# Seven products for eight in the FFN down projections of a two-layer decoder trunk

## The chip, the cores and the metric

One core of a Trainium2 chip runs the whole program. Five engines work side by side, each through its own queue in a fixed order: PE (matrix products), DVE (elementwise work), ACT (elementwise functions and copies), POOL (elementwise work) and SP (which issues DMA transfers). The metric is the device time of one execution in microseconds, as the median of several runs.

## The reference

The input is 512 tokens of width 1024 in float32. Two layers follow each other. Each is a mixer (attention in layer 0, causal pooling in layer 1) and then a SwiGLU feed-forward network (FFN), each between two RMS norms with a residual sum:

```python
def swiglu(h, w_gate, w_up, w_down):
    return (jax.nn.silu(h @ w_gate) * (h @ w_up)) @ w_down
...
        u = rmsnorm(h, g[2])
        h = h + rmsnorm(swiglu(u, ffn_w_gate[layer], ffn_w_up[layer], ffn_w_down[layer]), g[3])
```

The hidden width FFN_HIDDEN is 2816, which is 22 chunks of 128. The down projection is thus the product of a 512 x 2816 matrix of activations with a 2816 x 1024 matrix of weights.

## The kernel before

Every product is made from split numbers: `hi` is the operand rounded to fp32r, `lo` is the rest, and one product is three matmuls (hi by hi, hi by lo, lo by hi). To split one 128 x 512 tile, `conv` (line 242) lets ACT copy it into `hi` (line 244), and then DVE or POOL subtracts into `lo` (line 245). The engine of the subtraction comes from a pattern in CFG: the key `wlo` has 'ggv' (POOL, POOL, DVE) from the first FFN on, the key `slo` has 'v' (always DVE). `split` (line 219) is the same with DVE always.

An FFN has two parts. The gate and up projections (`Ffn.run`, `pair_weights`, `begin`, `middle`, `end`, `up_done`) go over 11 pairs of hidden chunks, first gate, then up for each pair, and already use a seven-product scheme: DVE combines weight blocks (line 913), ACT and DVE split them (lines 244, 245), PE multiplies with 256 columns at a time (lines 944 to 946), DVE puts the results together (lines 962 to 972) and makes the activations (lines 985 to 987). Two PSUM tags, psA and psS, with two banks each, hold these products.

The down projection follows (`down`, lines 776 to 813). It runs over two column halves n of 512. For each half it goes over the chunks, and in each chunk over the four token tiles of 128; one such step is three matmuls of 512 columns (lines 782 to 784), so 22 x 2 x 4 x 3 = 528 matmuls in a layer. Half 0 collects in the tags psT and psO, half 1 in psA and psS. Each weight tile is loaded, split once and used for four token tiles; each activation chunk is split once (`get`, line 1020). The last eight chunks of half 1 are kept back in a function `tail(t)`, which finishes token tile t, so that the norm of tile t (`post_norm`, line 815) can begin while PE works on tile t+1. In layer 0 the tails stand in the hand-written order `tr2` (line 62) with the pooling mixer: T is a tail, E is `Pool.enter` (post norm, then rows for the pooling), B the band matmuls (line 1126), M the mixing, F, R, A and Z prepare the next FFN, W its first weights. Before all of that `Pool.prepare` (line 1073) loads and scales the mixer's constants, lines 1079 and 1089 on DVE. In layer 1 the four tails are followed by the last norm and the store.

Tiles come from rotating groups by tag: `wq` (14 tiles of split weights), `wr` (11 raw weight tiles), `xe` (4), `g` (31, the general one), `jk` (2), `sc` (2). A tile can be written again only when its last reader is done. The order inside each engine's queue is set at build time by a planner that follows program order as priority and takes what is ready in its own time model.

## Time and profile before

| | |
|---|---|
| median of 3 runs | 1072.53 us (1071.33 to 1073.2) |
| the profiled execution | 1071.16 us |
| its span | 1069.4 us |
| PE busy | 1023.3 us, 96% |
| DVE busy | 755.3 us, 71% |
| ACT busy | 563.0 us, 53% |
| POOL busy | 314.5 us, 29% |

The span runs from the first to the last instruction. Times in the rows below count from the start of the span. Busy shares are means over stages that differ much from each other, so each stage is read by itself. Layer 0's down projection lies between 553 and 673 us, layer 1's between 943 and 1063 us.

### The profile page before, as it was taken

The numbers are of one execution on the slowest core, as the hardware profiler recorded it, in microseconds if no ns is written. First come the engines' busy times: TensorE is split into PE (matmuls) and PEld (weight loads), VectorE is DVE, ScalarE is ACT, GpSimd is POOL, SyncE is SP. The second block draws the span as 40 slices with busy tenths as digits, with TensorE's granted clock in tenths as the row PEclk, the third lists the DMA queues.
The fourth block names the chain that finished last, engine by engine and source line by source line (L and its number), as shares of the span: only waits on it lengthen the run. The fifth ranks groups of instructions, "written<-read, shape, count | busy, mean of one in ns | idle before, by whom it ended". The sixth has DMA issues, their size and how long they took to land.

```text
span 1069.4 us, 19004 instructions
## 1 busy us (share of the span) xinstructions
PE 1023.3 (96%) x6892; PEld 940.4 (88%) x6892; DVE 755.3 (71%) x1527; ACT 563.0 (53%) x1194; POOL 314.5 (29%) x282
## 2 busy tenths in 40 slices
PE   6999999997999999999999999988999999999997
PEld 5788978896888999999988888988999999978886
DVE  5338898758749999899973153998898898881204
ACT  6437688769656454454564352764444354472401
POOL 5713666767751000000026371420000000053510
PEclk9999999999999999999999999998999999999999
DMA  8841201323531434433343374003342333433302
GB/s 244 195 96 40 60 21 32 95 73 102 169 89 31 119 109 116 123 102 107 119 153 114 106 218 110 21 11 92 97 138 83 112 114 90 139 117 121 108 1 78
DMA packets 156493, 108.58 MB, mean 102 GB/s; under 512 B 14836, under 2 KB 137584, under 8 KB 156400
## 3 DMA queue, kind: packets, MB, share of 16 engines
q1 hardware_dynamic: 155600, 106.23, 34.6%
q8 instruction: 54, 0.88, 0.4%
q10 hardware_dynamic: 800, 1.15, 0.3%
q14 instruction: 39, 0.32, 0.1%
HBM read 101.88 MB, written 2.10 MB: 97 GB/s over the span
## 4 chain that ended last, share of the span: by engine, by line
PE 77%; DVE 8%; ACT 5%; issue 3%; DMA 3%; POOL 2%; SPq 1%; DVEq 0%; POOLq 0%; ACTq 0%
PE psS L944 8%; PE psS L945 8%; PE psS L946 7%; PE psA L944 5%; PE psA L945 5%; PE psA L946 5%; PE psT L784 2%; PE psO L784 2%; PE psT L782 2%; PE psT L783 2%; PE psO L783 2%; PE psO L782 2%; PE psA L782 2%; PE psA L784 2%; PE psA L783 2%
## 5 line engine op out<-in xcount | busy, mean ns | idle before, releaser
L244 ACT ACTIVATE wh<-wr 128x512 fp32r<-128x512 f32 x376 | 226.3, 626 | 256.8 <-DVE wr L913 82.4
L245 POOL TENSOR_TENSOR wl<-wr,wh 128x512 fp32r<-128x512 f32 x101 | 145.4, 1449 | 556.5 <-ACT wh L244 329.8
L245 DVE TENSOR_TENSOR wl<-wr,wh 128x512 fp32r<-128x512 f32 x275 | 189.5, 706 | 92.1 <-ACT wh L244 89.4
L944 PE MATMUL psS<-th,wh 128*128 128x256 f32 x528 | 149.8, 285 | 1.3 <-DVE comb L964 1.3
L945 PE MATMUL psS<-tl,wh 128*128 128x256 f32 x528 | 150.0, 285 | 0.0
L946 PE MATMUL psS<-th,wl 128*128 128x256 f32 x528 | 149.9, 284 | 0.0
L944 PEld LDWEIGHTS psS<-th,wh 128*128 128x128 f32 x528 | 101.6, 193 | 1.6 <-DVE comb L964 0.9
L945 PEld LDWEIGHTS psS<-tl,wh 128*128 128x128 f32 x528 | 101.8, 193 | 0.0
L946 PEld LDWEIGHTS psS<-th,wl 128*128 128x128 f32 x528 | 101.7, 193 | 0.0
L913 DVE TENSOR_TENSOR wr<-wr,wr 128x512 f32<-128x512 f32 x132 | 86.7, 682 | 1.3 <-DMA wr<-in_ffn_w_up_dram 0.5
L946 PE MATMUL psA<-uh,wl 128*128 128x256 f32 x272 | 77.5, 286 | 3.1 <-DVE wl L245 3.0
L944 PE MATMUL psA<-uh,wh 128*128 128x256 f32 x272 | 77.5, 286 | 2.1 <-DVE comb L962 1.7
L945 PE MATMUL psA<-ul,wh 128*128 128x256 f32 x272 | 77.3, 284 | 0.0
L270 POOL TENSOR_SCALAR E<-E,ri 128x128 f32<-128x128 f32 (+3 forms) x48 | 56.0, 1167 | 38.8 <-DVE ri L590 12.9
L584 ACT ACTIVATE E<-E,mn 128x128 f32<-128x128 f32 (+1 forms) x96 | 53.4, 557 | 15.7 <-DVE mn L582 15.0
L946 PEld LDWEIGHTS psA<-uh,wl 128*128 128x128 f32 x272 | 52.6, 194 | 3.5 <-DVE wl L245 3.5
L944 PEld LDWEIGHTS psA<-uh,wh 128*128 128x128 f32 x272 | 52.5, 193 | 2.7 <-DVE comb L962 2.1
L332 PE MATMUL psA<-uh,wh 128*128 128x512 f32 (+1 forms) x136 | 51.4, 378 | 1.7 <-DVE nq L464 1.5
L945 PEld LDWEIGHTS psA<-ul,wh 128*128 128x128 f32 x272 | 52.6, 193 | 0.0
L221 DVE TENSOR_TENSOR pl<-psT,ph 128x512 fp32r<-128x512 f32 (+1 forms) x72 | 42.3, 593 | 12.5 <-ACT ph L220 8.7
L334 PE MATMUL psA<-uh,wl 128*128 128x512 f32 (+1 forms) x136 | 50.9, 374 | 0.0
L333 PE MATMUL psA<-ul,wh 128*128 128x512 f32 (+1 forms) x136 | 50.7, 373 | 0.0
(354 smaller groups left out, 3009.8 us busy)
## 6 DMA issues: line engine op xcount, KB each, us to landing
wr<-in_ffn_w_gate_dram SPq DMA_DIRECT2D x98, 256.0 KB
wr<-in_ffn_w_up_dram SPq DMA_DIRECT2D x98, 256.0 KB
wr<-in_ffn_w_down_dram SPq DMA_DIRECT2D x88, 256.0 KB
wr<-in_attn_w_in_dram SPq DMA_DIRECT2D x40, 256.0 KB
wr<-in_attn_w_out_dram SPq DMA_DIRECT2D x16, 256.0 KB
x<-in_x_dram SPq DMA_DIRECT2D x4, 512.0 KB
gbc<-in_norm_g_dram SPq DMA_DIRECT2D x8, 256.0 KB
h<-in_x_dram SPq DMA_DIRECT2D x4, 512.0 KB
```

The costliest lines, as they stand in the source:

```text
L244: nc.scalar.activation(hi, src, AF.Copy)
L245: next_engine(key).tensor_tensor(lo, src, r32(hi), op=ALU.subtract)
L270: (nc.vector if k == "v" else nc.gpsimd).tensor_scalar(e, e, s1, None, op0=ALU.mult)
L332: nc.tensor.matmul(psum, wh, ah, start=first, stop=False)
L584: nc.scalar.activation(e, e, AF.Exp, bias=mn[:, n_:n_ + 1], scale=-1.0, accum_out=sm[:, n_:n_ + 1])
L782: nc.tensor.matmul(o, acts[c][0][:, tok], wh[k], start=first, stop=False)
L783: nc.tensor.matmul(o, acts[c][0][:, tok], wl[k], start=False, stop=False)
L784: nc.tensor.matmul(o, acts[c][1][:, tok], wh[k], start=False, stop=last)
L913: next_engine("sadd").tensor_tensor(o, x0, x1, op=op)
L944: nc.tensor.matmul(o, wh, bh, start=start and k == 0, stop=False, skip_group_check=True)
L945: nc.tensor.matmul(o, wh, bl, start=False, stop=False, skip_group_check=True)
L946: nc.tensor.matmul(o, wl, bh, start=False, stop=k == 3, skip_group_check=True)
```

## The change

Both down projections are rewritten as the method of the new class function `down(self, pairs)`. The tokens are cut into halves of 256, the hidden chunks into an even and an odd one of each pair, and the columns into halves of 512. Eight block products of a pair become seven (Strassen's scheme in Winograd's form). The first pass makes four products for each of the 11 pairs and collects them in four groups of two PSUM banks: C11 (psO), U (psT), C21 (psA), C12 (psS). Then the sums `u2` and `c22` are formed. The second pass makes the other three products of a pair and adds them onto C11, C21 and C12. The second-pass products of the last three pairs (`nres`) are kept back for the tails.

The scheme needs sums of blocks: three of half a tile for the activations (`act_sums`, made for the first six pairs, `npre`, already during the gate and up projections), four of weights, one more of activations. All splits of this stage use the key `slo`, so DVE makes every `lo`. Apart from this, the tag `sc` goes into `jk` (now 3), `g` has 33 tiles, and the two PSUM tags of the pooling mixer change places.

```diff
-    ng=31,
+    ng=33,
-    jk=2,
+    jk=3,
+    nres=3,
+    npre=6,
-    ptags=(('psO', 'psA'), ('psO', 'psS')),
+    ptags=(('psO', 'psS'), ('psO', 'psA')),
...
     def SC():
-        return T([P, S], "sc", 2, F32, "sc")
+        return JK("sc")
...
                     up_done(todo[i][0], ms[i - 1], ms[i])
+                    if pairs.index(todo[i][0]) < CFG["npre"]:
+                        self.act_sums(todo[i][0])
...
-            return down(get, NF, w_down[self.layer], lambda i: take)
+            return self.down(pairs)
+
+        def act_sums(self, p):
+            e, o = self.acts[2 * p], self.acts[2 * p + 1]
+            a11, a21, a22 = e[:, 0:256], e[:, 256:], o[:, 256:]
+            t_ = G([P, S], label="as")
+            s1, s3 = t_[:, 0:256], t_[:, 256:]
+            nc.vector.tensor_add(s1, a21, a22)
+            nc.vector.tensor_sub(s3, a11, a21)
+            nc.vector.tensor_sub(a21, s1, a11)
+            self.S[p] = t_
+
+        def down(self, pairs):
...
+            for i, p in enumerate(pairs):
+                if p not in self.S:
+                    self.act_sums(p)
+                b11, b12, b22 = raw(p, 0, 0), raw(p, 0, 1), raw(p, 1, 1)
+                t1, t2s[p] = JK("t1"), G([P, S], label="t2")
+                e_ = XE([P, 2, S], F32R, label="ae")
+                s_ = XE([P, 2, S], F32R, label="as")
+                conv(e_[:, 0, :], e_[:, 1, :], self.acts[2 * p], "slo")
+                w11 = put(b11)
+                sub(t1, b12, b11)
+                sub(t2s[p], b22, t1)
+                w2 = put(t2s[p])
+                sub(b12, b22, b12)
+                conv(s_[:, 0, :], s_[:, 1, :], self.S[p], "slo")
+                w3 = put(b12)
+                w1 = put(t1)
+                ends = i == 0, i == len(pairs) - 1
+                for o, a, c0, b in ((C11, e_, 0, w11), (U, e_, 256, w2), (C21, s_, 256, w3), (C12, s_, 0, w1)):
+                    for j in range(2):
+                        prod(o, (a[:, 0, c0:c0 + 256], a[:, 1, c0:c0 + 256]), b, j, *ends)
+            u2, c22 = [], []
+            for j in range(2):
+                x_ = G([P, S], label="u2")
+                nc.scalar.activation(x_, C11[j], AF.Copy)
+                nc.vector.tensor_add(x_, U[j], x_)
+                y_ = G([P, S], label="c22")
+                nc.vector.tensor_add(y_, C21[j], x_)
+                nc.vector.tensor_add(y_, C12[j], y_)
...
+            def second(p, keep):
+                b21, b22 = raw(p, 1, 0), raw(p, 1, 1)
...
+                w21 = put(b21, alloc)
...
+                conv(oh, ol, o, "slo")
+                sub(t2s[p], b21, t2s[p])
+                w4 = put(t2s[p], alloc)
+                sub(e[:, 256:], o[:, 0:256], e[:, 256:])
+                conv(s_[:, 0, :], s_[:, 1, :], e[:, 256:], "slo")
+                w22 = put(b22, alloc)
...
+            for p in pairs[:-R]:
+                for o, a, b in second(p, False):
+                    for j in range(2):
+                        prod(o, a, b, j)
+            held = [second(p, True) for p in pairs[-R:]]
+
+            def tail(t):
+                j = t % 2
+                for i, (p2, p4, p3) in enumerate(held):
+                    for x in ((p4,) if t >= 2 else (p2, p3)):
+                        prod(x[0], x[1], x[2], j, False, i == R - 1)
+                y_ = C([P, S], label="c12") if t < 2 else u2[j]
+                nc.vector.tensor_add(y_, (C12 if t < 2 else C21)[j], u2[j])
+                return [C11[j], y_] if t < 2 else [y_, c22[j]]
```

`put` is a split into two `wq` tiles (or into tiles that stay, for the held pairs), `sub` a DVE subtraction, `prod` three matmuls of 512 columns for one token tile.

## Rows read from the trace of the kernel before

**Rows 1.** Page, part 1: busy time of the engines over the span.
```profile
PE 1023.3 (96%) x6892; PEld 940.4 (88%) x6892; DVE 755.3 (71%) x1527; ACT 563.0 (53%) x1194; POOL 314.5 (29%) x282
```

**Rows 2.** Windows: start:end us, length, busy by engine (PE, PEld, DVE, ACT, POOL), clock, DMA.
```profile
362.00:553.00 191.00, 189.90 (x1583) 189.70 (x1581) 171.06 (x312) 93.13 (x167) 5.57 (x5) 1.00 0.41 118
553.00:673.00 120.00, 119.72 (x527) 98.85 (x528) 48.37 (x72) 50.47 (x94) 55.44 (x38) 1.00 0.45 132
673.00:740.00 67.00, 60.24 (x467) 58.24 (x465) 60.87 (x105) 42.56 (x88) 16.88 (x18) 0.90 0.10 28
943.00:1063.00 120.00, 119.79 (x528) 98.63 (x526) 37.10 (x52) 38.49 (x72) 38.77 (x29) 1.00 0.24 79
```

**Rows 3.** Timeline, PE: start us, length us, line, out<-in; idle before in brackets.
```profile
553.08 0.50 PE L782 MATMUL psT<-wh,ah 128*128 128x512 f32 x1 [1.17 <-ACT ah L220]
...
639.62 0.39 PE L783 MATMUL psA<-wl,ah 128*128 128x512 f32 x1
...
640.07 0.39 PE L782 MATMUL psS<-wh,ah 128*128 128x512 f32 x1
...
673.16 0.39 PE L784 MATMUL psS<-wrh,asp 128*128 128x512 f32 x1
```

**Rows 4.** Timeline, PE, layer 1's down projection: its first and its last matmul.
```profile
942.64 0.50 PE L782 MATMUL psT<-wh,ah 128*128 128x512 f32 x1 [1.17 <-ACT ah L220]
...
1062.73 0.39 PE L784 MATMUL psS<-wrh,asp 128*128 128x512 f32 x1
```

**Rows 5.** Timeline, DVE, back to back work in gate and up, and in down.
```profile
500.31 0.41 DVE L964 TENSOR_TENSOR comb<-psS,comb 128x256 f32<-128x256 f32 x1
500.64 0.68 DVE L245 TENSOR_TENSOR wl<-wr,wh 128x512 fp32r<-128x512 f32 x1
...
558.88 7.30 DVE L221 TENSOR_TENSOR al<-act,ah 128x512 fp32r<-128x512 f32 x12
```

**Rows 6.** Timeline, DVE, end of layer 0's gate and up, first and last of eight waits.
```profile
542.65 0.69 DVE L245 TENSOR_TENSOR wl<-wr,wh 128x512 fp32r<-128x512 f32 x1 [0.99 <-ACT wh L244]
...
551.94 0.69 DVE L972 TENSOR_TENSOR comb<-psS,comb 128x512 f32<-128x512 f32 x1 [1.50 <-PE psS L946]
```

**Rows 7.** Timeline, ACT, first and last down weight split before the down projection.
```profile
543.66 0.63 ACT L244 ACTIVATE wh<-wr 128x512 fp32r<-128x512 f32 x1 [1.05 <-DMA wr<-in_ffn_w_down_dram]
...
551.87 0.63 ACT L244 ACTIVATE wh<-wr 128x512 fp32r<-128x512 f32 x1 [0.81 <-PE psS L945]
```

**Rows 8.** Lines by form, 553 to 675 us: count, busy us, mean ns, idle before.
```profile
L1089 DVE SCALAR_TENSOR_TENSOR wr<-wr,gT,scbc 128x256 f32<-128x256 f32 x8 | 6.4, 862 | 0.0
L1079 DVE TENSOR_TENSOR band<-braw,band 128x128 fp32r<-128x128 f32 x4 | 2.0, 527 | 8.0 <-ACT band L1078 8.0
L245 POOL TENSOR_TENSOR wl<-wr,wh 128x512 fp32r<-128x512 f32 x22 | 38.1, 1742 | 31.6 <-ACT wh L244 31.5 <-DMA wr<-in_ffn_w_down_dram 0.2
```

**Rows 9.** Timeline, DVE, passage from layer 0 to layer 1.
```profile
641.72 1.78 DVE L245 TENSOR_TENSOR fwl<-wr,fwh 128x512 fp32r<-128x512 f32 x1
...
658.05 0.21 DVE L277 TENSOR_SCALAR ms<-sq 128x1 f32<-128x1 f32 x1 [10.48 <-ACT trash L818]
...
730.06 0.69 DVE L221 TENSOR_TENSOR tl<-psT,th 128x512 fp32r<-128x512 f32 x1 [1.24 <-ACT th L220]
```

**Rows 10.** Waits of PE, 673 to 745 us: total us, times, longest.
```profile
PE psA L946 <- DVE wl L245: 3.0, 1, 3.0
```

**Rows 11.** Window of 20 us, columns as in rows 2, with the lower clock.
```profile
720.00:740.00 20.00, 16.98 (x110) 15.89 (x108) 16.70 (x29) 9.41 (x17) 0.00 (x0) 0.71 0.18 53
```

**Rows 12.** Timeline, DVE and ACT, the last token tile in layer 1.
```profile
1063.94 0.21 DVE L277 TENSOR_SCALAR ms<-sq 128x1 f32<-128x1 f32 x1 [2.55 <-ACT trash L818]
...
1064.81 1.41 DVE L826 SCALAR_TENSOR_TENSOR h<-mq,rs,h 128x512 f32<-128x512 f32 x2
...
1066.26 0.34 ACTq L831 DMA_DIRECT2D out_dram<-h  x1
```

**Rows 13.** Lines by form, PE, whole span, columns as in rows 8.
```profile
L635 PE MATMUL psO<-PcT,VC 128*128 128x256 f32 x32 | 7.8, 309 | 1.4 <-ACT sc L652 1.4
```

More of the change, by code (lines that the diff above doesn't have):

```diff
@@ L1010, in run @@
             finish_(len(todo) - 1)
-            wres = T_([P, 8, S], "uh", 1, F32R, "wrh"), T_([P, 8, S], "ul", 1, F32R, "wrl")
-            pos = []
-            def take(shape):
-                pos.append(0)
-                k = len(pos) - 1
-                return tuple(w_[:, k:k + 1, :] for w_ in wres)
-            def get(c):
-                if c >= 20:
-                    t_ = XE([P, 2, S], F32R, label="asp")
-                    hi, lo = t_[:, 0, :], t_[:, 1, :]
-                else:
-                    f = G if c < 10 or c >= 16 else O if c < 14 else C
-                    hi, lo = (f([P, S], F32R, label=n_) for n_ in ("ah", "al"))
-                split(hi, lo, self.acts[c])
-                return hi, lo
@@ new lines, in down, with raw, put, sub @@
+        def down(self, pairs):
+            w = w_down[self.layer]
+            C11, U, C21, C12 = ([BANK(tag) for _ in range(2)] for tag in ("psO", "psT", "psA", "psS"))
+            def raw(p, k, n):
+                c = 2 * p + k
+                return load_raw(w[c * P:(c + 1) * P, n * S:(n + 1) * S].rearrange("(k p) f -> p k f", p=P), [P, 1, S])[0][:, 0, :]
+            def put(src, alloc=None):
+                hi, lo = alloc() if alloc else WQ2([P, S])
+                conv(hi, lo, src, "slo")
+                return hi, lo
+            def sub(o, x0, x1):
+                nc.vector.tensor_tensor(o, x0, x1, op=ALU.subtract)
+            def prod(o, a, b, j, first=False, last=False):
+                (ah, al), (bh, bl) = a, b
+                ah, al = ah[:, j * P:(j + 1) * P], al[:, j * P:(j + 1) * P]
+                nc.tensor.matmul(o[j], ah, bh, start=first, stop=False, skip_group_check=True)
+                nc.tensor.matmul(o[j], ah, bl, start=False, stop=False, skip_group_check=True)
+                nc.tensor.matmul(o[j], al, bh, start=False, stop=last, skip_group_check=True)
+            t2s = {}
+            for i, p in enumerate(pairs):
[26 more added lines that the diff above has]
+                nc.vector.tensor_add(y_, C12[j], y_)
+                u2.append(x_)
+                c22.append(y_)
+            def second(p, keep):
+                b21, b22 = raw(p, 1, 0), raw(p, 1, 1)
+                e, o = self.acts[2 * p], self.acts[2 * p + 1]
+                alloc = res_alloc if keep else None
+                o_ = XE([P, 2, S], F32R, label="ao") if not keep else G2()
+                s_ = G([P, 2, 256], F32R, label="s4")
+                w21 = put(b21, alloc)
+                if keep:
+                    oh, ol = o_
+                else:
+                    oh, ol = o_[:, 0, :], o_[:, 1, :]
+                conv(oh, ol, o, "slo")
[4 more added lines that the diff above has]
+                w22 = put(b22, alloc)
+                a12, a22 = ((oh[:, c0:c0 + 256], ol[:, c0:c0 + 256]) for c0 in (0, 256))
+                return (C11, a12, w21), (C21, a22, w4), (C12, (s_[:, 0, :], s_[:, 1, :]), w22)
+            def G2():
+                return tuple(G([P, S], F32R, label="aor") for _ in range(2))
+            wres = []
+            def res_alloc():
+                if not wres:
+                    for tag in ("uh", "ul"):
+                        t_ = T([P, 8, S], tag, 1, F32R, "wres")
+                        wres.extend(t_[:, k, :] for k in range(8))
+                    wres.append(None)
+                if wres[0] is None:
+                    return tuple(O([P, S], F32R, label="wro") for _ in range(2))
+                return wres.pop(0), wres.pop(0)
+            R = CFG["nres"]
+            for p in pairs[:-R]:
[11 more added lines that the diff above has]
+                return [C11[j], y_] if t < 2 else [y_, c22[j]]
+            return tail
```

1 line of the change is left out of this document (added).

## The prediction

> **What bounds the kernel now.** I read the page's busy shares first [rows 1]: PE 96%, DVE 71%. Then the windows by stage [rows 2]. In layer 0's gate and up stretch PE is full and DVE is busy for 171 of 191 us. [...] In the passage to layer 1 (673 to 740 us) DVE is busy for 61 of 67 us and PE for 60, so there DVE sets the pace as much. The reader is to see that the change takes work from PE exactly where PE is the bound, and hands work to DVE, which is the next engine in line, in a stretch enclosed by two others where DVE has little left.
>
> **What a matmul and a DVE operation cost.** A record's length is not what it costs in a full queue; the distance of starts is. Two down matmuls start 0.45 us apart over two steps, 0.227 us each, while their records say 0.39 [rows 3]; 528 of them are 119.7 us, the measured stretch. Twelve subtractions of 128x512 take 7.30 us with the last record of 0.68, so (7.30 - 0.68) / 11 = 0.602 us each; one of 128x256 is followed after 0.33 us [rows 5]. I take 0.60 and 0.335.
>
> **PE's part.** A pair of chunks had 2 x 2 x 4 x 3 = 48 matmuls and has 7 x 2 x 3 = 42. Over 11 pairs 528 become 462, a saving of 66 x 0.227 = 15.0 us in a layer, 30.0 us in both. This would be the gain if PE stayed the bound: 104.7 us of matmuls in a layer, of them 11 x 24 x 0.227 = 59.9 in the first pass, 8 x 18 x 0.227 = 32.7 in the second, and 54 x 0.227 = 12.2 in the tails.
>
> **DVE's part.** A pair in the first pass has six `lo` (e_, s_, w11, w2, w3, w1) and three weight sums, 9 x 0.602 = 5.42 us beside 5.45 us on PE. Five pairs still make their activation sums here, 5 x 3 x 0.335 = 5.0 us. Between the passes are six sums, 3.6 us. A pair in the second pass has four `lo` and one sum of 512 columns and two operations of 256, 5 x 0.602 + 2 x 0.335 = 3.68 us beside 4.09 us on PE. The sum is 11 x 5.42 + 5.0 + 3.6 + 11 x 3.68 = 108.7 us. That is more than PE's 104.7, and PE cannot end with it: the second pass of the last three pairs is wanted by every tail, so when DVE has made the last `lo` (I call this moment T), one held product of token tile 0 and the other three tails are still to run, 39 x 0.227 = 8.8 us. So DVE becomes the bound of the down stretch, and what counts is T.
>
> **DVE's lead.** How much of the 108.7 us is done before PE gets there? In the last 12 us of gate and up DVE waits eight times, 5.8 us together [rows 6], and it spends another 1.2 us on two `lo` of down weights, time that is just as free for the new down work. ACT gets its `wq` tiles for down weights between 543.7 and 551.9 us, seven of them [rows 7], and with the sums and activation splits they allow about 9 us of DVE work. I take a lead of 7 us (ends 0 and 9). Later the lead can't grow past about a pair, since `wq` has 14 tiles and a pair takes 8; the five late activation sums eat 5.0 of it. For waits inside the chain DVE, ACT, DVE (sum, hi, lo) the trace of before shows no such stage; I take 2 us of gaps in a layer, near the small waits where DVE is full in the passage, with ends 0 and 8 (the eight waits of rows 6 and some more).
>
> **Layer 1, term by term.** T = 942.6 [rows 4] - 7 + 108.7 + 2 = 1046.3. DVE then has for each token tile one sum (0.60), the small op (0.13), two products with g (1.2) and two residual updates (1.33) [rows 12], 4 x 3.27 = 13.1 us, starting 0.7 us after T, and the store takes 3.2 us from the last update to the end of the span [rows 12]: 1063.3. PE's own way gives 1046.3 + 8.8 + 6.3 (last matmul to end before) + 0.6 = 1062.0, so DVE's is taken: **-6.1 us** against 1069.4 (ends: -8 with no gap, +7 with no lead and 8 us of gaps).
>
> **Layer 0.** T = 553.1 [rows 3] - 7 + 108.7 + 2 = 656.8. Before, DVE's passage work begins at 658 and is solid, but for 6.7 us of waits, until the first wait behind 729 us [rows 9]: 64.3 us of work. Now four sums (2.4 us) come to it, and what DVE did for `Pool.prepare` in its idle time in the down stretch: eight scalings and four band splits [rows 8], without POOL beside them some 4 us, and two `lo` of 0.6. POOL's 22 `lo` of down weights go away [rows 8], which takes a disturbance from DVE: a `lo` beside POOL work took 1.78 us for 0.68 [rows 9]. But POOL's share of the mixer's and W0's weights now runs beside a full DVE, for which I add 2 us. 656.8 + 2.4 + 5.4 + 2 + 64.3 = 730.9 against 729, and of these 2 us the short DVE waits behind 730 us take most. **0 us** (ends -5 and +10). So layer 0 gains nothing, although PE has 15 us less to do there: the first band matmul starts right behind the last tail [rows 3], but its rows come from DVE.
>
> **Gate and up.** Six pairs' activation sums are 6 x 3 x 0.335 = 6.0 us more of DVE in a stretch with 20 us of DVE idle [rows 2]. The idle time hides most; I put **+0.8 us** a layer, 1.6 in all (ends 0 and 6.0 a layer, the whole of it, if DVE's idle time comes at the wrong places).
>
> **Edits at nothing.** Eleven more raw loads of 256 KB a layer: the DMA share is 0.45 and 0.24 in the down stretches [rows 2]; they queue on SP with the others, 11 `wr` tiles ahead. `sc` and `jk` together lose a tile in the attention: all of PE's idle time put down to such a copy is 1.4 us [rows 13], so 0, with 0 and +1.4 as ends. The changed PSUM tags only let the first band not wait for the last tails' banks.
>
> **The sum.** -6.1 + 0 + 1.6 = -4.5 on the profiled execution's 1071.16 gives 1066.7. That execution lies 1.4 us under the median of the runs shown, so the forecast is **1068.0 us**.
>
> [...] Starts 0.602 us apart with records of 0.68 [rows 5] say that DVE operations overlap a little. [...]
>
> **The rivals.** (1) DVE keeps ahead: the lead is used fully, the gaps are nil, the late activation sums and `Pool.prepare` find room in gate and up. Then PE is the bound, -13 us in layer 1 (15.0 less 2 at the seam of the passes) and -7 in layer 0, where the passage stays: 1052. For it: 9 us of DVE work are possible early; against it: DVE's total is over PE's. (2) DVE's queue stalls, the slower side: DVE works in a fixed order, so each sum that must pass through ACT and back, or a `wq` tile that PE still reads, holds everything behind it. Every us of gaps moves T, and T moves both layers' ends by as much. At 2 us of gaps the change gains 4.5; from about 4.3 us of gaps a layer on it loses. At 8 us: 12 us more, 1080. Against it: DVE runs without waits in much of the passage [rows 9]; for it: eight waits in 12 us where tiles come free slowly [rows 6]. [...] (3) DVE's operations cost their records when each waits for ACT: 160 x 0.68 + 37 x 0.41 = 124 us a layer instead of 108.7, 15 us more in both layers: 1098. Rows 5 speak against it, since there too each `lo` waits for an ACT copy.
>
> **How the numbers follow.** About 0.2%, 2.1 us, is what a measurement of this kernel can tell from no change: faster is under 1070.4, slower over 1074.7. Forecast 0.56 (1063 to 1074; of it 0.39 faster, 0.13 same, 0.04 slower); rival 1 0.14; rival 2 0.24 (0.05 same, 0.19 slower); rival 3 0.04; something else, 0.02, half faster, half slower. Faster 0.54, same 0.18, slower 0.28. The range reaches into rivals 1 and 2: 1054 to 1080.
>
> **What would show it.** Down stretches with DVE over 95% busy, PE waiting for `lo` by DVE, 924 matmuls of 512 columns instead of 1056, one PE wait of 3 to 5 us before the last held product of tail 0, a down stretch of about 112 us from first to last matmul. The forecast is wrong if PE is full through the first pass and the seam is short (rival 1), or if DVE shows waits on ACT of over 4 us a layer (rival 2).

## The result, and the profile after

The changed kernel takes 1118.71 us (median; 1112.25 to 1119.62) against 1071.93 us before (four runs each): a ratio of 1.0427 with an interval of 1.0383 to 1.0472. The forecast was 1068.0 us with a range of 1054 to 1080. The change makes the kernel slower, and the time lies 50.7 us above the forecast. The profiled execution took 1119.06 us, of it a span of 1117.0 us, where the span before was 1069.4.

Busy time by engine of the kernel after, the page's first part, against [rows 1]:

```profile
PE 1029.6 (92%) x6760; PEld 932.2 (83%) x6760; DVE 924.0 (83%) x1892; ACT 619.8 (55%) x1308; POOL 226.5 (20%) x223
```

DVE got 169 us more work (924.0 against 755.3) and POOL lost 88. The count of PE fell by 132, as planned, but its busy time rose. Matmuls that stand apart count with their whole record, 0.40 us for the first of the down projection below (462 of layer 0's make 111.4 us, 0.24 each, where a full queue takes 0.227), and the mean granted clock fell from 0.987 to 0.958.

Windows by stage of the kernel after (columns as in [rows 2]): layer 0's gate and up, its down projection, the gap ahead of the first band matmul, the passage, and layer 1's down projection.

```profile
358.00:568.00 210.00, 207.55 (x1696) 206.33 (x1697) 192.81 (x362) 96.49 (x175) 0.00 (x0) 0.98 0.38 110
568.30:688.20 119.90, 111.35 (x462) 85.29 (x461) 113.85 (x206) 72.98 (x135) 7.22 (x5) 0.99 0.47 143
688.20:699.10 10.90, 0.34 (x2) 0.00 (x0) 8.84 (x14) 5.41 (x12) 5.68 (x6) 0.72 1.04 279
699.10:769.20 70.10, 59.17 (x377) 55.75 (x377) 55.22 (x99) 40.43 (x86) 19.37 (x20) 0.77 0.04 10
986.50:1105.40 118.90, 109.50 (x458) 84.97 (x457) 110.94 (x201) 67.96 (x129) 0.55 (x1) 0.99 0.34 104
```

In both down stretches DVE is busy for 111 to 114 of 119 to 120 us, where it was 48 and 37 before and PE was busy for 119.7 and 119.8 of 120 us, at a granted clock of 1.00 [rows 2]. The stretches are hardly shorter than the 121.5 us of before. Behind layer 0's there are 10.9 us in which PE does next to nothing, and a passage in which the granted clock is 0.77 of full speed.

The same read as a table. Each boundary is the start of a matmul of the timeline: the last of the out projection, the first T product of layer 0's gate and up, the last of gate and up, the last of down, the first band matmul, the first T product of layer 1, the last of gate and up, the last of down, the end of the span. All times are us.

| Stretch | before | after | difference |
|---|---|---|---|
| start to last out projection | 316.7 | 328.1 | +11.4 |
| to first T product, layer 0 | 28.0 | 30.0 | +2.0 |
| rest of gate and up 0 | 206.9 | 210.2 | +3.3 |
| down 0 | 121.5 | 119.9 | -1.6 |
| gap to first band | 0.2 | 11.0 | +10.7 |
| passage to first T product, layer 1 | 52.6 | 70.1 | +17.4 |
| rest of gate and up 1 | 215.2 | 217.3 | +2.1 |
| down 1 | 121.5 | 118.9 | -2.7 |
| end | 6.6 | 11.6 | +5.0 |

Together +47.6 us, the difference of the spans. More than half of it lies where both kernels run the same matmuls: 13.4 us in the attention and 17.4 in the passage.

PE's timeline in the kernel after, layer 0's down projection and the first band, against [rows 3]:

```profile
568.36 0.40 PE L1053 MATMUL psO<-wl,ae 128*128 128x512 f32 x1
...
572.19 0.74 PE L1052 MATMUL psT<-wh,ae 128*128 128x512 f32 x2 [2.74 <-ACT wh L246]
...
680.45 0.39 PE L1054 MATMUL psS<-wro,s 128*128 128x512 f32 x1
...
688.16 0.39 PE L1054 MATMUL psA<-wres,aor 128*128 128x512 f32 x1
699.11 0.48 PE L1235 MATMUL psO<-band,vh 128*128 128x128 f32 x1 [10.56 <-ACT vh L1210]
```

and DVE's, the last `lo` of a held pair and the first sum of a tail, in layer 0 and in layer 1, and the last residual update ([rows 12]):

```profile
672.87 0.70 DVE L247 TENSOR_TENSOR wres<-t,wres 128x512 fp32r<-128x512 f32 x1
...
681.00 5.34 DVE L1198 SCALAR_TENSOR_TENSOR wr<-wr,gT,scbc 128x256 f32<-128x256 f32 x8
...
687.46 0.68 DVE L1136 TENSOR_TENSOR c<-psS,u 128x512 f32<-128x512 f32 x1
...
1090.88 0.69 DVE L247 TENSOR_TENSOR wres<-t,wres 128x512 fp32r<-128x512 f32 x1
...
1098.96 0.69 DVE L1136 TENSOR_TENSOR c<-psS,u 128x512 f32<-128x512 f32 x1 [3.80 <-PE psS L1054]
...
1112.47 1.42 DVE L828 SCALAR_TENSOR_TENSOR h<-mq,rs,h 128x512 f32<-128x512 f32 x2 [0.44 <-POOL rs L283]
```

The moment T of the prediction is 673.6 in layer 0 and 1091.6 in layer 1, 105.3 and 105.1 us behind the last gate and up matmul (568.24 and 986.46). The prediction's 656.8 and 1046.3 are 105.2 and 105.1 us behind the same matmul of before (551.6 and 941.2). So far it held. Layer 0's stretch up to T and behind it, in windows:

```profile
568.24:673.57 105.33, 96.78 (x398) 73.30 (x397) 104.91 (x192) 65.88 (x122) 0.00 (x0) 0.98 0.44 133
673.57:688.20 14.63, 14.63 (x67) 12.05 (x65) 8.94 (x15) 7.10 (x13) 7.22 (x5) 1.00 0.71 209
```

Up to T DVE is full, as forecast. Behind T PE is full and has 65 matmuls still to start (the window counts two more that began before it), where the prediction left it 39. So the last down matmul ends 15.0 us behind T in layer 0 and 14.2 in layer 1, instead of 8.8. The first tail's sum comes 7.4 us behind T in layer 1 and 13.9 us behind it in layer 0, instead of 0.7. In layer 1 it waits for PE. In layer 0 PE's last product of token tile 0 starts at 680.45, but the mixer's eight scalings stand ahead of the sum on DVE until 686.34, and two more `lo` behind them.

Layer 0's down projection in steps of 20 us (the same columns) shows where PE fell behind:

```profile
568.30:588.30 20.00, 17.26 (x69) 13.23 (x69) 19.64 (x34) 12.95 (x23) 0.00 (x0) 0.91 0.46 145
588.30:608.30 20.00, 20.00 (x90) 16.57 (x89) 20.00 (x38) 11.22 (x20) 0.00 (x0) 1.00 0.37 119
608.30:628.30 20.00, 18.36 (x77) 13.56 (x76) 20.00 (x40) 10.27 (x18) 0.00 (x0) 1.00 0.41 114
628.30:648.30 20.00, 16.58 (x63) 10.87 (x63) 20.00 (x36) 14.21 (x29) 0.00 (x0) 1.00 0.38 116
648.30:668.30 20.00, 19.40 (x83) 15.10 (x84) 20.00 (x39) 16.70 (x32) 0.00 (x0) 1.00 0.44 133
668.30:688.30 20.00, 19.85 (x88) 15.96 (x86) 14.21 (x25) 7.63 (x14) 7.32 (x5) 1.00 0.80 229
```

At 0.227 us each a full PE makes 88 matmuls in 20 us. In the first four steps, the first pass and the seam to the second, it makes 299 instead of 352 while DVE is full; in the last two, second pass and tails, PE is nearly full itself, and so makes up little. DVE is the bound up to T and PE behind it, and the two parts add.

### The profile page after: what moved, and what is told of

It is laid out like the page before. It is cut to its first block, busy times and chain, and to the rows that moved or that the text cites. A ratio compares the mean times of both kernels' runs of the same rounds, so it can differ in the third digit from the quotient of the medians.

```text
span 1117.0 us, 19288 instructions
## 1 busy us (share of the span) xinstructions
PE 1029.6 (92%) x6760; PEld 932.2 (83%) x6760; DVE 924.0 (83%) x1892; ACT 619.8 (55%) x1308; POOL 226.5 (20%) x223
## 4 chain that ended last, share of the span: by engine, by line
PE 65%; DVE 16%; ACT 7%; DMA 5%; issue 4%; POOL 2%; DVEq 0%; POOLq 0%; SPq 0%; ACTq 0%
PE psS L949 7%; PE psS L948 7%; PE psS L947 7%; PE psA L947 5%; PE psA L948 4%; PE psA L949 4%; DVE wl L247 3%; PE psO L637 2%; PE psS L579 1%; ACT wh L246 1%; PE psT L608 1%; DMA wr<-in_attn_w_in_dram 1%; PE psS L1052 1%; DVE h L828 1%; PE psA L334 1%
## 5 line engine op out<-in xcount | busy, mean ns | idle before, releaser
L247 DVE TENSOR_TENSOR wl<-wr,wh 128x512 fp32r<-128x512 f32 x326 | 222.6, 698 | 7.9 <-ACT wh L246 7.5
L247 POOL TENSOR_TENSOR wl<-wr,wh 128x512 fp32r<-128x512 f32 x54 | 71.9, 1344 | 383.9 <-ACT wh L246 380.9
L283 POOL TENSOR_TENSOR rs<-ms,mhalf 128x1 f32<-128x1 f32 x32 | 21.3, 667 | 413.7 <-DVE ms L279 380.0
L586 ACT ACTIVATE E<-E,mn 128x128 f32<-128x128 f32 (+1 forms) x96 | 53.4, 557 | 17.1 <-DVE mn L584 16.3
L947 PE MATMUL psA<-th,wh 128*128 128x256 f32 x176 | 50.4, 288 | 3.0 <-ACT comb L957 3.0
L948 PEld LDWEIGHTS psA<-ul,wh 128*128 128x128 f32 x272 | 52.6, 193 | 0.0
```

The lines of the kernel that those rows point to most:

```text
L247: next_engine(key).tensor_tensor(lo, src, r32(hi), op=ALU.subtract)
L283: nc.gpsimd.tensor_tensor(rs, ms, mhalf, op=ALU.pow)
L586: nc.scalar.activation(e, e, AF.Exp, bias=mn[:, n_:n_ + 1], scale=-1.0, accum_out=sm[:, n_:n_ + 1])
L947: nc.tensor.matmul(o, wh, bh, start=start and k == 0, stop=False, skip_group_check=True)
L948: nc.tensor.matmul(o, wh, bl, start=False, stop=False, skip_group_check=True)
```

## The experiments

Differences by stretch in this section are against the table's column for before. The attention, where most kernels are alike, took 312.9 to 319.5 us from its start to the last out projection in executions of kernels that leave it alone, so there a difference under 4 us is not read. The passage is steadier: 52.5 to 52.7 us in four kernels below that share it with before.

**e1: only the tile groups.** Three lines change: `sc` goes into `jk`, `jk` has 3 tiles, `g` has 33.

```
 def SC():
-    return T([P, S], "sc", 2, F32, "sc")
+    return JK("sc")
-ng=31, jk=2
+ng=33, jk=3
```

> The kernel before with only the change of tile groups: the copies of `finish` take their tile from jk (3 tiles) instead of sc (2) beside jk (2), and g has 33 tiles; no seven-product down projection. Theory A (the 11 us by which the attention is longer in the changed kernel come from the shared tiles): the out projection's last matmul at about 327 us instead of 316, and 1081 to 1085 us in all. Theory B (they come from how the planner orders the queues when work behind the attention changes): the attention as before, 1071 to 1074 us.

1094.6 us, ratio 1.0228 (1.0208 to 1.0249): 8.3 and 2.0 us more up to the first T product, and 9.5 us more in the passage, with not one matmul taken away. Theory A is right about the place; the time is above its 1081 to 1085 us, since it did not count on the passage. The window from 120 to 140 us in before, in after and in e1, in this order:

```profile
120.00:140.00 20.00, 20.00 (x118) 17.00 (x117) 16.37 (x52) 13.96 (x39) 11.08 (x10) 1.00 0.18 51
```
```profile
120.00:140.00 20.00, 16.68 (x88) 13.84 (x88) 11.21 (x31) 9.16 (x26) 8.65 (x10) 0.91 0.30 80
```
```profile
120.00:140.00 20.00, 16.68 (x83) 14.10 (x83) 12.29 (x36) 9.52 (x27) 7.60 (x8) 0.83 0.19 53
```

PE goes from full to 16.68 of 20 us in both, and no engine takes its place: DVE, ACT and POOL all do less. That reads as a chain through several engines which has become longer, not as a busy engine. The attention's loss comes with the tile groups; e9 parts them.

**e2: the change with `sc` in two tiles of its own.**

```
 def SC():
-    return JK("sc")
+    return T([P, S], "sc", 2, F32, "sc")
-ng=33, jk=3
+ng=32, jk=2
```

> The changed kernel with sc as a group of its own again (2 tiles), jk 2 and g 32, the seven-product down projections in both layers. Theory A: the attention is back at before's length and the time falls by 11 us to about 1107. Theory B: it stays at 1116 to 1121, or moves in the attention by some other amount.

1102.71 us, ratio 1.0306 (1.0286 to 1.0325). The attention is back (-1.3 and 0.0), as theory A says, and the passage loses 11.8 instead of 17.4 us. The rest stays: +3.5 and +2.5 in gate and up, -2.1 and -0.4 in down, 11.9 ahead of the first band, +4.7 at the end. The next experiments start from e2.

**e3 and e4: seven products in one layer.** Each has e2's `sc`, and the old down projection in the other layer.

```
+            if self.layer in CFG["seven"]:      # e3: (1,)   e4: (0,)
+                return self.down(pairs)
```

> Seven products in layer 1's down projection alone, eight in layer 0, tile groups as in the run before this one, the mixer's PSUM tags as before. From the stretches of the changed kernel: 2.6 us saved between the last gate and up matmul and the last down matmul, 5.4 us more behind it, little in gate and up: 1073 to 1078 us if what follows layer 0's down projection is what costs (theory C). If DVE's added work costs alike in both layers (theory D): 1085 to 1092.

> Seven products in layer 0's down projection alone, eight in layer 1. Theory C: the passage from layer 0 to layer 1 takes 25 to 30 us more, its first band matmul waits 8 us or more behind the last tail and the clock is low for over 20 us there: 1095 to 1105 us. Theory D: 1085 to 1092.

e3 takes 1085.43 us, ratio 1.0139 (1.0118 to 1.0161): layer 1 alone loses 2.5 in gate and up, wins 0.5 in down and loses 5.0 at the end. But 5.9 us are lost in the passage, which lies behind the old down projection and in front of all new work. e4 takes 1094.02, ratio 1.0221 (1.0203 to 1.0240): +3.5, -2.1, +12.4 ahead of the bands, +11.8 in the passage. So neither layer gains, and something reaches the passage that is not the new work. The times do not decide between the theories: e3's falls into D's range, e4's between the two ranges.

**e5: no early activation sums** (`npre=0`): all eleven pairs make theirs in the down projection, 18 small DVE operations a layer more there.

> Seven products in both layers with sc as its own group (the run e2, 1102.7 us), and no activation sums in the gate and up projections (npre 0): DVE makes all of them in the down stretch, 6.0 us more there. Theory E (DVE's total sets the down stretch, and the early sums cost PE in gate and up): gate and up back to 207 and 215 us from 210.4 and 217.6, the down stretches 4 to 6 us longer than 119.4 and 121.2; 1102 to 1106 us. Rival (PE loses time in the down stretch by the order of DVE's work, not by its amount): the down stretches stay within 1 us, 1096 to 1099.

1110.2 us, ratio 1.0372 (1.0349 to 1.0395). Gate and up are back at 206.7 and 213.0 us, 3.8 and 4.6 under e2. The down stretches grow to 128.4 and 128.8, 9.0 and 7.6 over e2. The windows of layer 0's, e2 first and then e5:

```profile
553.90:673.30 119.40, 109.03 (x459) 85.16 (x457) 114.93 (x207) 71.91 (x135) 6.80 (x5) 0.99 0.46 140
```
```profile
550.30:678.60 128.30, 113.56 (x464) 84.77 (x463) 123.08 (x228) 73.42 (x137) 7.07 (x5) 0.97 0.44 133
```

DVE's busy time rises by 8.2 us and the stretch by 8.9, with the same matmuls. DVE's amount of work sets this stretch. Stretch and time came out above theory E's 4 to 6 us and 1102 to 1106: the sums cost 8.2 us there, priced at 6.0.

**e6: a third of the `lo` of the down projection on POOL.**

```
+    dlo='vvg',
-                conv(hi, lo, src, "slo")
+                conv(hi, lo, src, "dlo")
```

> As e2, but POOL makes every third lo of the down stretch (key dlo, pattern 'vvg'), 36 of 110 a layer, 22 us less for DVE by its back to back cost. Theory E: the down stretches fall from 119.4 and 121.2 to 108 to 113 us, 1085 to 1094 in all. Rival (a DVE operation beside POOL work takes 1.78 instead of 0.68 us, so each lo on POOL costs DVE as much as it takes away): the down stretches stay at 119 to 124.

1148.05 us, ratio 1.0721 (1.0700 to 1.0742): down takes 140.8 and 145.9 us, far over both forecasts. Layer 0's down projection, to be read against e2's above:

```profile
555.40:696.20 140.80, 117.75 (x458) 90.73 (x457) 127.12 (x169) 73.57 (x136) 91.30 (x46) 0.92 0.41 124
```

Groups of lines in and right behind layer 0's down projection (count, busy us, mean ns, idle before):

```profile
L248 POOL TENSOR_TENSOR wl<-t,wh 128x512 fp32r<-128x512 f32 x25 | 60.8, 2449 | 252.9 <-ACT wh L247 249.4 <-PE psT L1055 2.9 <-POOL wl L248 0.4
...
L248 POOL TENSOR_TENSOR wl<-wr,wh 128x512 fp32r<-128x512 f32 x8 | 11.6, 1444 | 13.9 <-ACT wh L247 11.4 <-PE psS L1055 2.4
```
```profile
L248 DVE TENSOR_TENSOR wl<-wr,wh 128x512 fp32r<-128x512 f32 x34 | 31.0, 913 | 0.9 <-ACT wh L247 0.8
```

and the same of DVE in e2:

```profile
L247 DVE TENSOR_TENSOR wl<-wr,wh 128x512 fp32r<-128x512 f32 x39 | 27.8, 719 | 0.0
```

A `lo` on POOL takes up to 2449 ns in the mean, and the ones that stay on DVE 913 instead of 719 in e2. DVE has fewer operations in the stretch than in e2 (169 against 207) and is busy for 12 us longer. Work moved off the full engine made it slower; by what mechanism, no run shows.

**e7: the mixer's preparation behind the first two post norms.**

```
-    pool.prepare()
+    pool.gains()
-tr2='W0 T0 T1 E0 T2 E1 B0 ...
+tr2='W0 T0 T1 E0 T2 E1 P B0 ...
```

> As e2, but the pooling mixer's preparation (its loads, band splits, eight scalings of weights) stands in program order behind the first two post norms, ahead of the first band, and only its norm gains stand ahead. Theory F (in e2 the first post norm waits in DVE's queue behind the mixer's preparation, whose loads wait for tiles): the first band matmul waits 4 to 8 us behind the last tail instead of 12.1, and 1092 to 1099 in all. Rival (the preparation itself is what the bands wait for, wherever it stands): 12 us or more, 1102 to 1108.

1105.95 us, ratio 1.0331 (1.0314 to 1.0348). PE's wait ahead of the first band is 15.8 us, and it is now for the band rows themselves:

```profile
PE psO L1237 <- ACT band L1190: 15.4, 1, 15.4
```

So the rival is right: the preparation can't simply go behind, the bands need it.

**e8: no `lo` of the down projection's weights.** That takes 77 operations a layer from DVE. It also leaves each such weight one `wq` tile instead of two, so weights can be made further ahead; the two are not parted.

```
-                hi, lo = alloc() if alloc else WQ2([P, S])
-                conv(hi, lo, src, "slo")
-                return hi, lo
+                hi, lo = alloc() if alloc else (WQ([P, S], "wh"), None)
+                nc.scalar.activation(hi, src, AF.Copy)
+                return hi, hi
```

> As e2, but the lo of the down weights is left out: hi is read in its place, so PE's 462 matmuls stay and DVE has 77 subtractions less a layer, 46 us of 109. Theory E: PE becomes the bound, the down stretches are 105 to 109 us. Rival (the order of the passes, banks or ACT hold PE up): 114 us or more.

1081.14 us, one execution and so without an interval. Windows of layer 0's down projection, of the gap ahead of the bands and of the passage:

```profile
557.50:667.40 109.90, 106.22 (x458) 87.48 (x457) 72.84 (x135) 74.35 (x139) 8.45 (x6) 0.97 0.56 169
```
```profile
667.60:675.40 7.80, 0.17 (x2) 0.01 (x1) 6.05 (x10) 3.99 (x9) 3.57 (x4) 0.84 0.47 141
675.40:740.80 65.40, 53.41 (x377) 50.93 (x377) 55.28 (x99) 39.67 (x84) 19.62 (x20) 0.81 0.06 17
```

With DVE at 73 us the two down stretches are 11.6 and 12.7 us shorter than before: most of the 15.0 us a layer of the prediction's PE part. With e5 that puts the length of the down stretch on DVE's work there. But the gap ahead of the bands is still 8.0 us (12.1 in e2), the passage 65.4 and the end 11.5 us long, though DVE is nowhere near full in the stretch in front. For the end, which in layer 1 has no mixer behind it, that rules out DVE's load in the stretch. For the gap it does not rule out DVE's queue: behind the sum of tile 0 DVE here waits twice for the gain of the post norm, 5.7 us in all:

```profile
663.68 0.69 DVE L824 TENSOR_TENSOR mq<-psO,gbc 128x512 f32<-128x512 f32 x1 [3.35 <-DMA gbc<-in_norm_g_dram]
666.71 0.69 DVE L824 TENSOR_TENSOR mq<-c,gbc 128x512 f32<-128x512 f32 x1 [2.35 <-DMA gbc<-in_norm_g_dram]
```

**e9 and e10: one tile more, nothing else**, each against the kernel before.

```
-    jk=2            # e9
+    jk=3
```
```
-    ng=31           # e10
+    ng=32
```

> The kernel before with one edit: three jk tiles instead of two; sc keeps its own two tiles and all 528 matmuls of each down projection stay. It parts the number of tiles from their sharing in e1. Theory S (what cost 8.3 us in the attention and 9.5 us in the passage of e1 is that sc and jk wait for each other's tiles): attention and passage stay as before, 1070 to 1074 us. Rival N (any other number of tiles changes the order of the work that the planner writes out, and with it the passage): the attention stays, the passage grows by 5 to 10 us, 1077 to 1082 us.

> The kernel before with one edit: 32 g tiles instead of 31. In e3 layer 0 is the one of before and still the passage is 5.9 us longer; besides layer 1's own operations only this number of tiles differs. Rival N (the number of tiles changes the planner's order in the passage): the passage grows by some 6 us, 1076 to 1080 us. Theory L (layer 1's new operations or loads reach back into the passage): the passage stays at 52.6 us, 1070 to 1074 us.

e9 takes 1079.56 us, ratio 1.0057 (1.0034 to 1.0080); the attention stays up to the last out projection (+0.1), and the passage is 2.7 us longer. The other 5.6 us lie in +2.3 up to the first T product and +1.0 and +2.3 in gate and up. So e1's 8.3 us are not the third `jk` tile; they come with the sharing (33 `g` tiles were not tried alone; 32, in e10, cost 2.0 there, under what is read). e1's 2.0 up to the first T product come with the third `jk` tile alone. e10 takes 1078.35, ratio 1.0046 (1.0028 to 1.0064), and its passage is 6.4 us longer. The passage of before and of e10:

```profile
673.40:726.00 52.60, 47.52 (x377) 45.90 (x376) 49.77 (x88) 36.48 (x78) 16.48 (x18) 0.92 0.07 20
```
```profile
675.40:734.40 59.00, 50.99 (x377) 49.43 (x376) 49.24 (x87) 35.28 (x75) 15.76 (x17) 0.86 0.05 15
```

The same 377 matmuls and the same DVE work, one more `g` tile, and 6.4 us, where the number of tiles can only act through the planner's order and the waits for free tiles. It is as much as e3's loss in the passage (5.9, with 32 `g` tiles too), and likely a part of the losses there in the other kernels with other tile numbers.

**e11: the band rows' raw loads in `jk` tiles**, not behind `xe` tiles that the second pass holds (e2 otherwise).

```
-                raw = XE([P, 3, P], label="braw")
+                raw = JK("braw", 3 * P).rearrange("p (b c) -> p b c", b=3)
```

> e2 with one edit: the four raw loads of the band rows go into jk tiles instead of xe tiles, which the second pass of the down projection holds. Theory Q (the bands come 12 us late because their loads wait on the SP queue for xe tiles, with the mixer's weights, scales and gains queued behind them): the wait ahead of the first band falls from 11.9 us to under 4, and 1091 to 1096 us. Rival D (the loads are not what is late, it is the queue of DVE): the wait stays over 8 us, 1099 to 1103 us.

1104.18 us, ratio 1.0291 (1.0264 to 1.0318). PE still waits 11 us ahead of the bands, so the band rows' loads were not what was late (the gain of the post norm stays in the SP queue where it was):

```profile
PE psO L1235 <- ACT vh L1210: 10.8, 1, 10.8
```

**e12: seven products in six of the eleven pairs.** The other five run plainly in the second pass, and the last two of these are what the tails hold, 24 matmuls a token tile as before the change; tile numbers as before, band rows as in e11.

```
-            for i, p in enumerate(pairs):
+            for i, p in enumerate(pairs[:X]):       # X = nx = 6, first and second pass
...
+            mid = pairs[X:-2]                       # plain, second pass
+            held = [plain(p, True) for p in pairs[-2:]]
```

> Seven products in six of the eleven pairs of chunks of each down projection, eight in the other five, whose products run in the second pass and, for the last two pairs, in the tails; the band rows in jk tiles; tile numbers as before the change (31 g, 2 jk, sc with its own). 492 matmuls a layer, 111.7 us of PE by 0.227 us each, against about 80 us of DVE by the prediction's prices, instead of 108.7. Theory E (in the change DVE is the bound of the down stretches, so the saved matmuls show only where DVE has room): both stretches take 112 to 115 us instead of 121.5, the end stays at 6.6 us, gate and up lose 1 to 2 us; with a passage between 53 and 60 us the whole takes 1058 to 1066 us. Rival W (the two passes themselves, their seam and the new order cost what is saved): the stretches take 118 us or more, 1070 us or more.

1076.74 us, ratio 1.0026 (1.0007 to 1.0045). The gap ahead of the bands is gone (0.2 us), the end is 7.5 us, the passage 58.2. The down stretches are 118.6 and 118.2 us, longer than the 112 to 115 that I expected of them:

```profile
554.40:673.10 118.70, 113.75 (x489) 92.80 (x487) 99.40 (x172) 68.79 (x129) 13.59 (x12) 0.97 0.51 153
```

DVE has 99 us here and not 80, and it is full in the first 60 us (59.5 busy), as in after. On the stretch and the time the rival was right, on the end nearly the theory (+0.9). Two things differ from e2 at the gap: the tails are long, and the mixer's scalings run from 631.4 to 639.1 us and the loads of the gains are issued from 640.2 on, ahead of the tails, where in e2 they come at 666.0 and 671.6 us, among the tails.

**e13: short tails alone.** The kernel before, with four chunks instead of eight left to the tails.

```
-            ntail = 0 if n == 0 else 8
+            ntail = 0 if n == 0 else nh     # nh = 4 in the FFN, else 8
```

> The kernel before, all 528 matmuls of each down projection, with one edit: four chunks of the second column half are left to the tails instead of eight, so a tail is 12 matmuls, 2.7 us, instead of 24, 5.4 us, and 36 instead of 72 matmuls lie between tail 0 and the first band. Theory H (in the change it is the short tails that no longer cover the post norm of tile 0, and at the end the four post norms): PE waits 5 to 10 us ahead of the first band, the end grows from 6.6 to 8 to 10 us, 1080 to 1095 us. Rival (the tails have slack enough; what is late in the change is DVE's queue): both stay within 1 us, 1070 to 1076 us.

1091.01 us, ratio 1.0177 (1.0140 to 1.0214). It costs about 20 us to do the same matmuls with less of them behind tile 0; the time lies in theory H's range. But the place is another than I wrote: PE doesn't wait ahead of the first band (0.2 us), and the end grows by 0.3 us only. The passage is 16.1 us longer. Its window, and the longest wait of PE in it:

```profile
674.90:743.70 68.80, 52.76 (x373) 50.79 (x371) 52.46 (x94) 39.43 (x83) 16.80 (x19) 0.87 0.03 8
```
```profile
685.38 0.58 PE L1142 MATMUL psO<-fwh,ph 128*128 128x256 f32 x1 [4.53 <-DVE mq L822]
```

DVE is busy for 52.5 of 68.8 us, where it was 49.8 of 52.6: PE now waits for post norms that before ran under the tails. Some 6 us of the 16 can be another order, as in e10; the other 10 are more than a tile's number cost anywhere here.

That there is no gap matters for the change, since here too 36 matmuls lie behind tile 0. The statistic of tile 0 in layer 0 and its first row for the bands, then the first statistic and the last residual update of layer 1:

```profile
667.70 0.21 DVE L277 TENSOR_SCALAR ms<-sq 128x1 f32<-128x1 f32 x1 [7.75 <-ACT trash L818]
...
672.08 0.72 ACT L1101 ACTIVATE vh<-h,rs 128x512 fp32r<-128x512 f32 x1
...
1075.15 0.21 DVE L277 TENSOR_SCALAR ms<-sq 128x1 f32<-128x1 f32 x1 [24.08 <-ACT trash L818]
...
1084.43 1.42 DVE L826 SCALAR_TENSOR_TENSOR h<-mq,rs,h 128x512 f32<-128x512 f32 x2
```

DVE has waited for tile 0, and the row follows 4.4 us behind the statistic, before the last tail ends. The four norms of layer 1 take DVE 10.7 us. In the kernel after the sum of tile 0 comes 7.0 us behind its last product, the first band 11.6 us behind the sum, and the four norms of layer 1 take DVE 14.9 us (1098.96 to 1113.89), four sums of 0.6 us and 1.6 us of waits for POOL's `rs` more.

**e14: two pairs held instead of three** (`nres=2` in e2): tails of 12 and 6 matmuls instead of 18 and 9.

> e2 with one edit: two pairs of the second pass are held for the tails instead of three, 12 and 6 matmuls a tail instead of 18 and 9, so 24 instead of 36 lie behind tail 0. Theory H (short tails): the band wait grows from 11.9 us by up to 2.7 us and the end by 1 to 2 us, 1104 to 1110 us. Rival (DVE is late, and less held work lets it end earlier): the band wait falls, 1096 to 1102 us.

1105.35 us, ratio 1.0325 (1.0304 to 1.0345). The gap ahead of the bands grows from 12.1 to 15.4 us and the end from 11.4 to 13.0, while DVE in the down stretch is busy for 113 instead of 115 us. PE's wait in e2 and in e14, and DVE's waits for the post norm's gain in e14:

```profile
PE psO L1235 <- ACT vh L1210: 11.7, 1, 11.7
```
```profile
PE psO L1235 <- ACT vh L1210: 15.0, 1, 15.0
```
```profile
679.90 0.69 DVE L824 TENSOR_TENSOR mq<-psO,gbc 128x512 f32<-128x512 f32 x1 [1.39 <-DMA gbc<-in_norm_g_dram]
...
682.98 0.69 DVE L824 TENSOR_TENSOR mq<-c,gbc 128x512 f32<-128x512 f32 x1 [2.39 <-DMA gbc<-in_norm_g_dram]
```

Twelve matmuls less behind tile 0 are 2.7 us by 0.227; the wait grew by 3.3. But in e14 DVE waits 3.8 us for the gain and in e2 0.4, a difference as large, so e14 doesn't show that the gap follows the tails. For the end the tails are shown to matter: it is 7.5 us with 72 matmuls behind tile 0 (e12), 11.4 with 36 (e2), 13.0 with 24, and a DVE with time to spare does not shorten it (e8). They don't act alone: in e13, with 36 matmuls and shorter norms, it is 6.9. The gap's cause stays open between the cover, the late scalings and the late gain, which all changed together from e2 to e12; e13 speaks against the cover alone.

**e15 and e16: e12's projection in layer 1 alone**, with the tile numbers and layer 0 of before; e16 without early activation sums.

```
+    seven=(1,), nx=6, npre=3        # e15
+    seven=(1,), nx=6, npre=0        # e16
```

> e12's down projection (seven products in six of eleven pairs, long tails of 24 matmuls) in layer 1 alone; layer 0 and the numbers of tiles as before the change. Theory: layer 0, gate and up and the passage stay as before since neither their operations nor the tiles differ; the down stretch of layer 1 is 3.4 us shorter as in e12, the end 0.9 us longer, gate and up 0.6 us: 1069 to 1071 us, at or just under before. Rival (any edit upsets the order that the planner writes for the passage): 5 us more there, 1074 to 1078 us.

> e15 with one edit: no activation sums in gate and up; all six pairs make theirs in the down projection, 3 pairs x 3 x 0.335 = 3 us more of DVE there. Theory: gate and up come back by 0.6 us, and the first pass, in which DVE is full, gives 1 to 3 us back: 1069 to 1073 us. Rival (DVE's room in the second pass takes it up): 1068 to 1070 us.

e15 takes 1070.66 us, ratio 0.9996 (0.9975 to 1.0018). The passage is that of before, 52.7 us, as the theory says: with the tiles unchanged the planner's order there is unchanged. Layer 1 gets 3.4 us in down and gives back 1.1 at the end and 1.4 in gate and up. e16 takes 1073.64, ratio 1.0017 (0.9996 to 1.0037), by its theory's 1069 to 1073 just missed. In its profiled execution, with 1068.68 us near the shortest of ten, the down stretch is 122.8 us, 4.6 longer than e15's, for 3 us of activation sums moved into a first pass in which DVE is full.

**e17 and e18: eight and four pairs** in layer 1 (`nx=8`, `nx=4`).

> e15 with eight of eleven pairs in seven products instead of six: 480 matmuls in layer 1's down projection, 109.0 us of PE instead of 111.7. Theory (in the first pass DVE, 5.42 us and an activation sum a pair, is as long as PE, 5.45 us, so each more pair there costs what it saves): the stretch of layer 1 takes 117 to 119 us as in e15, 1069 to 1072 us. Rival (DVE's room in the second pass pays for it): 2.7 us less, 115 to 116 us, 1067 to 1069 us.

> e15 with four of eleven pairs in seven products: 504 matmuls, 114.4 us of PE. Theory (the loss in e15 is PE's start, where DVE has no lead, and grows with the first pass): the stretch of layer 1 takes 117.5 to 119 us, 1069 to 1072 us. Rival (DVE sets e15's length and is relieved here): 115 to 117 us, 1067 to 1069 us.

e17 takes 1070.76 us against 1072.44 of before on the same chip, ratio 0.9980 (0.9967 to 0.9993): a gain of 0.2%, just on the bound of what can be told, and the only one of a kernel with all its products. Its down stretch, 118.7 us, is no shorter than e15's with 12 matmuls less. e18 left out one plain pair of chunks against my expectation, so it ran 456 matmuls and not 504, and its 1060.76 us, ratio 0.9892 (0.9871 to 0.9913), leave out 48 x 0.227 = 10.9 us of PE and the splits of that pair. With these matmuls alone its stretch would be an estimated 107.8 + 10.9 = 118.7 us. Layer 1's down projection in e15, e17 and e18:

```profile
942.70:1060.80 118.10, 114.04 (x492) 92.53 (x491) 89.31 (x156) 56.44 (x107) 1.64 (x3) 0.99 0.33 103
```
```profile
942.80:1061.60 118.80, 113.22 (x481) 89.69 (x479) 100.81 (x182) 61.16 (x117) 1.65 (x3) 0.99 0.34 106
```
```profile
942.50:1050.30 107.80, 105.12 (x457) 86.13 (x455) 72.31 (x124) 47.82 (x91) 1.65 (x3) 0.98 0.32 98
```

Four, six and eight pairs come out alike, within the estimate for e18. That fits the theory that a pair costs again, in a first pass where DVE has no lead, what it saves on PE; no run parts this from PE's wait at the start of the pass.

## Why the prediction was wrong, point by point

**PE's part** was right: 0.227 us a matmul, 462 in a layer, and e8 shows 12 of the 15 us when DVE has 77 operations less to make.

**DVE's part** was right as a total. T came when it was forecast, counted from the end of gate and up, with DVE busy for 104.9 of the 105.3 us up to it, so the 2 us of gaps that the prediction adds were not there; that the sum met T within 0.2 us is in part luck. e5 confirms that DVE's amount sets the length. Rivals 1 and 3 fall with this: DVE didn't keep ahead, and its operations didn't cost their records end to end.

**What lies behind T** was the first failed step. I compared 108.7 and 104.7 over the whole stretch, and let PE end 8.8 us, 39 matmuls, behind T. But the passes are unlike: in the first DVE has as much as PE or more, so PE falls behind by 53 matmuls, 12 us, the seam included; in the second PE has more, so it can't catch up. PE had 65 matmuls, 14 to 15 us, left at T. The bounds belong to passes, and they add.

**Layer 0's way from T to the bands** was the second failed step, and the worst, since no rival had it. I wrote that three tails still run behind tile 0 and priced them as PE time, 8.8 us. Before, 72 matmuls or 16.3 us behind tile 0 hid the post norms; now 36 do. I priced the mixer's scalings and splits behind T as 5.4 us of DVE and not as a wait of the first band, whose chain they stand in; before, the scalings ran from 624.9 to 631.9 us, under PE's products. I put DVE's passage work as one solid block of 64.3 us behind T, but in the passage after DVE is busy for only 55 of 70 us: it stands in a chain with ACT and PE. Layer 0's term was 0 with ends -5 and +10; it measured -1.6 + 10.7 + 17.4 = +26.5. Layer 1's was -6.1; it measured -2.7 + 5.0 = +2.3: the first sum came 6.7 us later behind T than I had put it, since PE had more left, and the four norms took 14.9 us instead of 13.1. Layer 1's end is shown to be short tails against a longer norm of each tile (e8, e12, e13, e14). Of layer 0's gap the runs show the parts, 7.0 us from tile 0's last product to its sum and 11.6 from there to the first band, but not which change would close it: short tails, late scalings and a late gain come together.

**The passage** is settled in part. Of its 17.4 us, 5.6 go with the tile groups (e2 against after). One more `g` tile alone makes 6.4 (e10), so a part is likely the planner's order, which the prediction took as given. The 5.4 us between e10's 6.4 and e2's 11.8 may come with the short tails, which e13 shows to cost 16.1 in before; with long tails and the old tile numbers 5.5 us are left (e12). No run adds these parts up. How much of it is the lower clock stays open: from 699.1 us on PE's granted clock is 0.77 of full speed in the mean of 70.1 us, 0.50 from 699 to 712 us, and PE had stood still for 10.6 us ahead of it.

**`sc` and `jk`** were the third failed step, a term of the sum: 0, with +1.4 as the end. It measured 13.4 us up to the first T product, and by e1 10.3 of it with the tile groups alone: 8.3 with the sharing, and 2.0 that a third `jk` tile alone makes too (e9). I had taken the idle time of PE that is put down to the copy [rows 13]. That row tells what PE waits for now, not what other engines will wait for when a tile is given to two users.

**Gate and up** measured +5.4 for +1.6, inside its ends of 0 and 12. In layer 0 it is the early sums (e5 is back at 206.7). In layer 1 they are one cause, since e1 and e9 lose 1.9 and 2.3 us there without any. The sum of the four misses (`sc` and `jk`, gate and up, layer 0, layer 1) is 13.4 + 3.8 + 26.5 + 8.4 = 52.1 us, which is the span's 1117.0 against the forecast's 1064.9.

**What was priced at nothing:** the raw loads and the SP queue. The band rows' loads are indeed nothing (e11). The post norm's gain, in the same queue, is not: DVE waits for it 0.9 us in after, 3.8 in e14 and 5.7 in e8.

**Rival 2** had the sign, and not the mechanism: up to T DVE's queue hardly stalls (idle for 0.4 of 105.3 us). The range stopped at 1080 because each term had its own ends, and those of layer 0 and of `sc` and `jk` did not reach far enough.

## What to carry to other kernels

Before work is moved to the next engine, compare the engines pass by pass and not over the stretch: where one is full in the first half and the other in the second, the shortfalls add. Ask of each block that a change shortens what ran underneath it, and of each block that it moves who waits for it: in e13 36 matmuls less behind tile 0 cost about 20 us with no work changed. In a kernel whose order a planner writes, a tile count or a shared tile is an edit of its own: try it alone first, as three such lines here cost 2.3% together (e1) and one more tile alone 0.5% (e10) or 0.6% (e9).

## What was not expected of the hardware

POOL and DVE hurt each other more than the trace of before tells: with a third of the `lo` on POOL, one took up to 2449 ns there in the mean of a group, against 1742 in before [rows 8], and DVE's own went from 719 ns in e2 to 913 (e6). And the passage's time did not follow the granted clock: the same passage took 52.6 us at 0.92 in before and 52.7 us at 0.96 in e15, with DVE busy for 49.8 and 49.9 us:

```profile
673.40:726.10 52.70, 46.69 (x378) 45.37 (x376) 49.86 (x88) 36.38 (x78) 16.49 (x18) 0.96 0.07 20
```
